# One layer of a hybrid decoder trunk: the q, k, sc_C and sc_x projections with stationary activations and blocks of quarters

## The chip, the core and the metric

One core of a Trainium2 chip runs the whole kernel in one launch. Its engines are TensorE (PE; the loading of its stationary operand has records of its own, PEld), VectorE (DVE), ScalarE (ACT), GpSimd (POOL) and SyncE (SP), which here only issues transfers. The metric is device time in microseconds (us), the median of three runs; lower is better.

## The reference

A batch of one, 256 tokens, 2048 channels, one layer, all in float32. What matters here:

```
h = rms_norm(x, norm_mix_g)                      # 256 x 2048
proj = h @ w_in                                  # 2048 x 14336
q, k, v, xr, gr, sc_b, sc_c, sc_x, g_pre = split(proj)   # 8 pieces of 1024, then 3 x 2048 gates
A = attention(q * 128**-0.5, k, v, rel_table)    # 8 heads of 128, causal, relative-position bias
B = rg_lru(conv4(xr)) * gelu(gr)                 # recurrence along the tokens
C = sc_b * conv3(sc_c * sc_x)                    # causal, per channel
m = sig(g_A) * (A @ w_attn_o) + sig(g_B) * (B @ w_lru_o) + sig(g_C) * (C @ w_sc_o)
x = x + m @ w_out
x = x + relu(rms_norm(x) @ w_up)**2 @ w_down     # 2048 -> 8192 -> 2048
return rms_norm(x) * final_g
```

## The kernel before

**Products in parts.** Each float32 number is split into a part `hi` in a shorter format (fp32r) and the rest `lo`; a product is hi·hi + hi·lo + lo·hi. The activations h are kept split (16 blocks `h0` to `h15` of 128 channels; the first 256 columns hi, the next 256 lo). Weights come from memory in tiles `raw` of 128x1024 (two blocks of 128 input channels by 512 output columns, 512 KB). One tile to be multiplied is called a job: `in_parts` writes hi by a copy on ACT and lo by a subtraction on DVE, both 128x1024, in a ring of WB = 5 buffers each. `ahead(n)` writes the program so that parts are made LOOK = 3 jobs ahead of the products.

**Two ways to multiply.** `group` (`ws`) keeps the weights stationary: for each 128x128 block of weights one matmul of 512 columns (hi against h in both parts) and one of 256 (lo against the hi part of h). A group is 512 output columns, 8 jobs; the result stands with channels on the partitions, its two parts are added (`total`: an ACT copy, a DVE addition, 256 columns each) and scaled by the norm's factor per token, `rsb`. `pair` (`as`) keeps the activations stationary and multiplies two groups at once: 12 matmuls of 512 columns per job, 16 jobs; the result stands with tokens on the partitions.

**Blocks of quarters.** In a pair, `nb` blocks of four jobs are multiplied by a scheme of seven products instead of eight (as Strassen's): `as_sequence` gives the order of the steps s1 to s7 and of the plain jobs n1, n2. Of such a block PE does seven half jobs (6 matmuls each) instead of four jobs (12 each); in return seven parts are made instead of four, and steps 2, 3, 4 and 6 first add two raw tiles on DVE (line 192). The stationary side of steps 2 to 5 needs sums of h, which `sums` makes on DVE and ACT (`h0c`, `h1c` and their parts). Steps 3 and 4 end in two more DVE operations (lines 309 and 310), and the final results of three of the four quarters need one more addition.

**Order of the work.** xr (two groups), q, k (two groups each, `ws`), v (a pair without quarters), sc_C, sc_x (`ws`), then for each branch its factor, the gates (`gt`, pairs with two blocks) and its output projection (`y`), then `wo`, and four times `up` and `dn`. Small work is written as generators put `beside` the products: `prepare` (tables for the bias: a matmul `pr`, its copy `rsbuf`, then through memory to POOL's tiles `rh` and `rl`, flipped by the matmuls `pf`), `recurrence`, `attention`, `h_sums`. `a_bit` runs one piece of the first generator in line, at most `pace` of them, and one entry of `after`, the rest of an evacuation (for xr: a multiplication by `rsb`, an ACT copy and three DVE multiply-adds for each of 8 pieces of the convolution). Only SP's order is the program's; that of the other engines is fixed when the program is built, by a scheduler. Each engine works off its own list in order.

Of the kernel before, what the change touches and what calls it, by code (L numbers as in the profile page):

```python
# [62 lines left out]
def trunk_kernel(ctx, tc, x8, xn, pv, rows, w_in, rel, onehot, w_a, lru_w, w_l, w_s, w_out, w_up, w_down, out2):  # L63
# [207 lines left out]
    def pair(name, w, g, plain, mix, evac, late=0):  # L271
# [41 lines left out]
        for n, s in enumerate(seq):  # L313
# [246 lines left out]
    pair("v", w_in, 4, lambda k, t: in_two(hl[k], t), None, evac)  # L560

    def attention():
        pt, pT = {}, {}
# [46 lines left out]
    hm = {}  # L610

    def h_sums():
        for b in range(NB_GATE):
            a = [block(f"ha{b}{i}") for i in range(2)]
            for i in range(4):
                h = hl[4 * b + i].bitcast(F32)
                dve.tensor_add(half(a, i), h[:, :S], h[:, S:])
            hm[b] = sums(f"h{b}", *a)
            yield

    beside(h_sums())
# [3 lines left out]
    sc = []
    for gidx in range(2):
        def evac(j, ps, gidx=gidx):
            g = 4 * gidx + j
            if g % 2 == 0:
                sc.append(block(f"sc{g}"))  # L630
            b = total(ps, f"sc{g}")
            dve.tensor_mul(half(sc, g), b, rsb)
        group(f"sc{gidx}", w_in, 12 + gidx, hl, evac)
    for gidx in range(2):
        def evac(j, ps, gidx=gidx):
            g = 4 * gidx + j
            b = total(ps, f"sx{g}")

            def rest():
                dve.tensor_mul(b, b, rsb)  # L640
                xp = u256(f"sp{g}", S + 2)
                dve.memset(xp[:, :2], 0.0)
                c = half(sc, g)
                dve.tensor_mul(xp[:, 2:], b, c)
# [289 lines left out]
```

## Time and profile before

| | |
|---|---|
| time, median of 3 runs (lowest, highest) | 1573.79 us (1573.08, 1576.48) |
| the profiled execution, its own time | 1573.67 us |
| its span, first to last instruction | 1571.9 us |
| PE busy | 1543.2 us (98%) |
| DVE busy | 1279.7 us (81%) |
| ACT busy | 878.5 us (56%) |
| mean granted TensorE clock | 0.997 |

The profiled execution's time is its span and 1.8 us around it, and 0.1 us below the median. PE's busy time holds the modelled ends of pipelined matmuls; how fast PE really goes is read from a run of matmuls without a gap.

### The profile page before, as it was taken

What the parts mean: (1) busy time and instruction counts of PE and PEld (TensorE: products, weight loads), DVE (VectorE), ACT (ScalarE), POOL (GpSimd) and SP (SyncE); (2) the same over time, 40 slices, a digit from 0 to 9 for tenths busy, and PEclk for the clock granted to TensorE, in tenths of its full rate; (3) what the DMA queues carried; (4) which work ended last, traced back from release to release, by engine and by line L of the source; (5) the groups of instructions that cost most, each with busy time, mean ns of one, the idle gap of its engine ahead of it and who ended that gap; (6) DMA issues with size and microseconds to landing.
All of it is one profiled execution on the core that took longest, in us unless ns stands there. A gap on an engine that the chain in (4) does not pass through costs nothing.

```text
span 1571.9 us, 20794 instructions
## 1 busy us (share of the span) xinstructions
PE 1543.2 (98%) x7684; PEld 1298.2 (83%) x7684; DVE 1279.7 (81%) x1649; ACT 878.5 (56%) x1172; POOL 57.2 (4%) x70
## 2 busy tenths in 40 slices
PE   8999999999999999999999999999999999999996
PEld 6888888878888888878788888888888888888885
DVE  6775566999769886989899778977799679976897
ACT  6555866565446454656557556545555446545554
POOL 1021200000000000200000000000000000000000
PEclk9999999999999999999999999999999999999998
DMA  9765555375755575473765654675467554666453
GB/s 360 254 196 170 162 189 160 121 271 160 245 182 175 188 268 183 135 268 128 262 202 187 214 189 139 208 254 188 134 214 252 187 185 171 195 236 209 145 183 112
DMA packets 87574, 309.77 MB, mean 197 GB/s; under 512 B 10269, under 2 KB 10533, under 8 KB 87472
## 3 DMA queue, kind: packets, MB, share of 16 engines
q1 hardware_dynamic: 83808, 298.67, 56.9%
q0 software_dynamic: 2656, 8.45, 1.9%
q8 instruction: 60, 0.98, 0.3%
q10 hardware_dynamic: 1008, 1.32, 0.2%
q14 instruction: 42, 0.34, 0.1%
HBM read 306.30 MB, written 2.11 MB: 196 GB/s over the span
## 4 chain that ended last, share of the span: by engine, by line
PE 84%; DVE 10%; issue 3%; DMA 1%; ACT 1%; POOL 0%; DVEq 0%; SPq 0%; POOLq 0%; ACTq 0%
PE dn L298 18%; PE up L251 15%; PE y L298 8%; PE up L252 8%; PE gt L298 8%; PE wo L298 5%; DVE lo L160 5%; PE qk L251 4%; PE v L298 3%; PE qk L252 2%; PE sc L251 2%; PE sx L251 2%; DVE raw L192 2%; PE xr L251 2%; PE sb L251 1%
## 5 line engine op out<-in xcount | busy, mean ns | idle before, releaser
L159 ACT ACTIVATE hi<-raw 128x1024 fp32r<-128x1024 f32 x648 | 667.4, 1056 | 554.1 <-DVE raw L192 115.5
L160 DVE TENSOR_TENSOR lo<-raw,hi 128x1024 fp32r<-128x1024 f32 x648 | 774.6, 1224 | 230.3 <-ACT hi L159 214.2
L251 PE MATMUL up<-h,hi 128*128 128x512 f32 x1024 | 360.5, 397 | 0.0
L252 PE MATMUL up<-h,lo 128*128 128x256 f32 x1024 | 287.5, 281 | 0.0
L251 PEld LDWEIGHTS up<-h,hi 128*128 128x128 f32 x1024 | 192.2, 188 | 46.4
L298 PE MATMUL dn<-hi,U 128*128 128x512 f32 x704 | 221.7, 389 | 0.4 <-ACT hi L159 0.4
L252 PEld LDWEIGHTS up<-h,lo 128*128 128x128 f32 x1024 | 193.5, 189 | 0.1
L298 PE MATMUL gt<-hi,h 128*128 128x512 f32 x528 | 167.9, 391 | 2.1 <-ACT hi L159 1.9
L298 PEld LDWEIGHTS dn<-hi,U 128*128 128x128 f32 x704 | 132.1, 188 | 28.6 <-ACT hi L159 0.8
L192 DVE TENSOR_TENSOR raw<-raw,raw 128x1024 f32<-128x1024 f32 x128 | 153.2, 1217 | 0.8
L298 PE MATMUL dn<-lo,U 128*128 128x512 f32 x352 | 137.2, 390 | 1.2 <-DVE lo L160 1.2
L298 PEld LDWEIGHTS gt<-hi,h 128*128 128x128 f32 x528 | 99.0, 188 | 23.9 <-ACT hi L159 2.9
L298 PE MATMUL gt<-lo,h 128*128 128x512 f32 x264 | 103.6, 392 | 3.0 <-DVE lo L160 3.0
L251 PE MATMUL qk<-h,hi 128*128 128x512 f32 x256 | 91.5, 401 | 0.0
L298 PEld LDWEIGHTS dn<-lo,U 128*128 128x128 f32 x352 | 66.1, 188 | 15.4 <-DVE lo L160 2.0
L252 PE MATMUL qk<-h,lo 128*128 128x256 f32 x256 | 71.7, 280 | 0.0
L298 PEld LDWEIGHTS gt<-lo,h 128*128 128x128 f32 x264 | 49.6, 188 | 16.0 <-DVE lo L160 5.6
L251 PEld LDWEIGHTS qk<-h,hi 128*128 128x128 f32 x256 | 48.1, 188 | 12.2 <-ACT hi L159 0.6
L251 PE MATMUL xr<-h,hi 128*128 128x512 f32 x128 | 45.3, 409 | 7.3 <-DVE h L379 6.7
L252 PEld LDWEIGHTS qk<-h,lo 128*128 128x128 f32 x256 | 48.3, 189 | 0.3
L251 PE MATMUL sc<-h,hi 128*128 128x512 f32 x128 | 46.6, 403 | 0.0
L251 PE MATMUL sx<-h,hi 128*128 128x512 f32 x128 | 45.9, 401 | 0.0
(899 smaller groups left out, 2315.9 us busy)
## 6 DMA issues: line engine op xcount, KB each, us to landing
raw<-in_w_in SPq DMA_DIRECT2D x222, 512.0 KB, 4.3
raw<-in_w_up SPq DMA_DIRECT2D x128, 512.0 KB, 4.3
raw<-in_w_down SPq DMA_DIRECT2D x128, 512.0 KB, 4.3
raw<-in_w_out SPq DMA_DIRECT2D x32, 512.0 KB, 4.5
raw<-in_w_a SPq DMA_DIRECT2D x16, 512.0 KB, 4.7
raw<-in_w_s SPq DMA_DIRECT2D x16, 512.0 KB, 5.3
raw<-in_w_l SPq DMA_DIRECT2D x16, 512.0 KB, 5.3
gb<-in_rows POOLq DMA_DIRECT2D x12, 256.0 KB, 4.6
```

Of the source, the lines that this page charges most:

```text
L159: act.activation(hi, raw, AF.Copy)
L160: dve.tensor_sub(lo, raw, hi.bitcast(F32))
L192: dve.tensor_add(t, t, add)
L251: pe.matmul(ps[j], hi[:, kk, cs], acts[k], start=(k == 0), stop=False)
L252: pe.matmul(ps[j][:, :S], lo[:, kk, cs], acts[k][:, :S], start=False, stop=(k == nk - 1))
L298: pe.matmul(ps[key], hl_[x], w2[y][:, kk], start=key not in begun, stop=end and i == 2, skip_group_check=True)
```

## The change

q, k, sc_C and sc_x go from `group` to `pair`, with 2, 1, 1 and 1 blocks of quarters; v gets one block. q and k come out with tokens on the partitions and are turned by `turned` (four 128x128 transposes on PE into one bank) and copied on ACT; the product of sc_C and sc_x is formed with tokens on the partitions and turned, too. The sums of h are formed beside the second half of xr's products, ahead of `prepare`, not beside sc_x's. In `as_sequence` step 7 stands behind step 4, with a plain job between steps 3 and 4; `dn` begins with its last plain jobs. There is one raw buffer less (8), six more blocks (49), and three small pools become one of 8.

```diff
-NBLK = 43
+NBLK = 49
-RAW = 9
+SMALL = 8
+RAW = 8
-NB_V, NB_Y = 0, 0
+NB_Q, NB_K, NB_V, NB_SC, NB_SX, NB_Y = 2, 1, 1, 1, 1, 0
...
+    units = list(range(2 * nb, nu))
+    if turn:
+        units = units[2:] + units[:2]
...
-    head = s[1] + n2[:a] + s[5] + s[2] + n2[a:-1] + s[3] + s[7] + s[4] + n2[-1:]
+    head = s[1] + n2[:a] + s[5] + s[2] + n2[a:-2] + s[3] + n2[-2:-1] + s[4] + s[7] + n2[-1:]
...
-    order = [("ws", w_in, g, 0, 8, 0) for g in (6, 7, 0, 1, 2, 3)]
-    order.append(("as", w_in, 4, 0, 8, NB_V))
-    for br, (w, gs) in enumerate(((w_a, (12, 13, 14, 15)), (w_s, (10, 11)), (w_l, (8, 9)))):
+    order = [("ws", w_in, g, 0, 8, 0) for g in (6, 7)]
+    order += [("as", w_in, g, 0, 8, nb) for g, nb in ((0, NB_Q), (2, NB_K), (4, NB_V), (12, NB_SC), (14, NB_SX))]
+    for br, (w, gs) in enumerate(((w_a, ()), (w_s, (10, 11)), (w_l, (8, 9)))):
...
+    def turned(name, o0, o1, j):
+        ps = small(name)
+        for q in range(2):
+            for th, src in ((0, o0), (1, o1)):
+                at = (2 * q + th) * P
+                pe.transpose(ps[:, at:at + P], src[:, (2 * j + q) * P:(2 * j + q + 1) * P], ident)
+        return ps
...
+    def h_sums():
+        for _ in range(4):
+            yield
+        for b in range(2):
...
+    beside(h_sums())
     A, B, C = [], [], []
     beside(prepare())
...
+        def evac(t, i, ps, other, op, which=which):
+            o = on[t, i] = block(f"qn{which}{t}{i}")
+            if other is not None:
+                dve.tensor_tensor(o, ps, other, op=op)
+                ps = o
+            act.activation(o, ps, AF.Copy, scale=rs1[:, S + t:S + t + 1] if which else rsq[:, t:t + 1])
...
+            def rest():
+                for j in range(2):
+                    n = 4 * which + 2 * i + j
+                    qk[n] = block(f"qk{n}")
+                    act.activation(qk[n], turned(f"pq{n}", o0, o, j), AF.Copy)
+            return rest
...
+        pair(f"qk{which}", w_in, 2 * which, lambda k, t: in_two(hl[k], t), hm, evac)
```

What moves on DVE at the beginning of q. The list of DVE before, from the fourth job of q on; `xc` is xr's convolution, `xp` its input:

```order
L498 SCALAR_TENSOR_TENSOR xc0_594<-xp0_591,pvt_77,xc0_594 128x256
L492 TENSOR_TENSOR xp1_659<-xr1b_374,rs1_166 128x256
L160 TENSOR_TENSOR lo19_673<-raw19_670,hi19_672 128x1024
L355 TENSOR_TENSOR xr6b_645<-xr1_2_402,xr6a_643 128x256
L498 SCALAR_TENSOR_TENSOR xc0_594<-xp1_659,pvt_77,xc0_594 128x256
L160 TENSOR_TENSOR lo20_679<-raw20_676,hi20_678 128x1024
```

And in the changed program, in the middle of q (jobs 25 to 30, steps 3 and 4; `raw21_01` and `raw22_01` are the raw tiles that step 4 adds to):

```order
L161 TENSOR_TENSOR lo25_808<-raw17_00_604,hi25_807 128x1024
L161 TENSOR_TENSOR lo26_820<-raw26_817,hi26_819 128x1024
L523 SCALAR_TENSOR_TENSOR xc4_776<-xp5_835,pvt_77,xc4_776 128x256
L193 TENSOR_TENSOR raw21_01_708<-raw21_01_708,raw19_11_673 128x1024
L523 SCALAR_TENSOR_TENSOR xc4_776<-xp5_835,pvt_77,xc4_776 128x256
L193 TENSOR_TENSOR raw22_01_729<-raw22_01_729,raw20_11_686 128x1024
L523 SCALAR_TENSOR_TENSOR xc4_776<-xp5_835,pvt_77,xc4_776 128x256
L161 TENSOR_TENSOR lo27_844<-raw21_01_708,hi27_843 128x1024
L161 TENSOR_TENSOR lo28_856<-raw22_01_729,hi28_855 128x1024
L310 TENSOR_TENSOR qk03_865<-qk0_10_847,qk0r1_698 128x512
```

The convolution, which stood among single subtractions, now stands among subtractions, additions of raw tiles and the ends of the steps.

The copy `rsbuf`, with which the tables for the bias begin, on DVE before (behind the eighth job of q):

```order
L160 TENSOR_TENSOR lo23_806<-raw23_803,hi23_805 128x1024
L498 SCALAR_TENSOR_TENSOR xc2_717<-xp3_766,pvt_77,xc2_717 128x256
L454 COPY rsbuf_775<-pr_773 8x384
L498 SCALAR_TENSOR_TENSOR xc2_717<-xp3_766,pvt_77,xc2_717 128x256
L160 TENSOR_TENSOR lo24_812<-raw24_809,hi24_811 128x1024
```

And in the changed program (behind step 6 of q, jobs 33 and 34; q's last job is 37):

```order
L193 TENSOR_TENSOR raw16_00_526<-raw16_00_526,raw29_10_876 128x1024
L193 TENSOR_TENSOR raw17_00_604<-raw17_00_604,raw30_10_894 128x1024
L574 TENSOR_TENSOR qn001_968<-qk0_01_715,qk03_865 128x512
L161 TENSOR_TENSOR lo33_942<-raw16_00_526,hi33_941 128x1024
L161 TENSOR_TENSOR lo34_953<-raw17_00_604,hi34_952 128x1024
L574 TENSOR_TENSOR qn011_971<-qk0_11_722,qk04_925 128x512
L464 COPY rsbuf_976<-pr_974 8x384
L161 TENSOR_TENSOR lo35_1007<-raw35_1004,hi35_1006 128x1024
```

It moved from the first half of q to its end, behind all of the convolution and all the additions.

DVE beside xr, before (the tenth and eleventh jobs; `sc8` are tiny operations of `prepare`):

```order
L355 TENSOR_TENSOR xr2b_386<-xr0_2_170,xr2a_384 128x256
L355 TENSOR_TENSOR xr3b_398<-xr0_3_171,xr3a_396 128x256
L442 TENSOR_SCALAR sc8_167<-sc8_167 128x8
L441 TENSOR_TENSOR sc8_167<-sc8_167 128x8
L442 TENSOR_SCALAR sc8_167<-sc8_167 128x8
L443 TENSOR_TENSOR sc8_167<-sc8_167 128x8
L160 TENSOR_TENSOR lo10_349<-raw10_346,hi10_348 128x1024
```

And in the changed program, at the same place:

```order
L365 TENSOR_TENSOR xr3b_381<-xr0_3_171,xr3a_379 128x256
L516 MEMSET xp0_579 128x3
L494 TENSOR_TENSOR ha00_437<-h0_98 128x256
L494 TENSOR_TENSOR ha00_437<-h1_105 128x256
L161 TENSOR_TENSOR lo10_332<-raw10_329,hi10_331 128x1024
L494 TENSOR_TENSOR ha01_438<-h2_115 128x256
L494 TENSOR_TENSOR ha01_438<-h3_121 128x256
L101 TENSOR_TENSOR h0c_443<-ha00_437 128x2x128
L99 TENSOR_TENSOR h0c_443<-ha00_437,ha01_438 128x2x128
L161 TENSOR_TENSOR lo11_393<-raw11_390,hi11_392 128x1024
```

The sums of h, 16 operations of 256 columns and two of 1024 in all, now stand between xr's ninth and last job.

## Rows read from the trace of the kernel before

**Rows 1.** The page, its first parts: span, busy time of the engines, and the granted clock in 40 slices of the span (tenths of full speed).

```profile
span 1571.9 us, 20794 instructions
PE 1543.2 (98%) x7684; PEld 1298.2 (83%) x7684; DVE 1279.7 (81%) x1649; ACT 878.5 (56%) x1172; POOL 57.2 (4%) x70
PEclk9999999999999999999999999999999999999998
```

**Rows 2.** Stretches of the span, in order: xr; q; k; v; sc_C; the first gates; sb; the fifth and the sixth pair of gates. Columns: stretch, its length, busy time (and count) of PE, PEld, DVE, ACT, POOL, granted clock, share of the DMA engines, GB/s.

```profile
0.00:55.70 55.70, 47.93 (x258) 40.67 (x259) 36.32 (x80) 37.66 (x68) 5.20 (x13) 1.00 0.95 351
55.70:104.60 48.90, 48.90 (x275) 41.69 (x274) 40.88 (x70) 25.89 (x38) 12.10 (x13) 1.00 0.64 201
104.60:153.50 48.90, 48.90 (x275) 42.67 (x274) 24.85 (x33) 23.75 (x37) 5.77 (x5) 1.00 0.56 176
153.50:198.90 45.40, 45.40 (x201) 37.57 (x201) 26.97 (x28) 35.66 (x51) 10.37 (x7) 1.00 0.54 170
198.90:253.20 54.30, 54.30 (x318) 46.96 (x316) 36.51 (x79) 34.41 (x71) 0.00 (x0) 1.00 0.53 169
303.20:346.60 43.40, 41.87 (x181) 33.38 (x180) 43.00 (x53) 27.29 (x32) 0.00 (x0) 1.00 0.57 188
431.00:476.30 45.30, 45.30 (x258) 39.24 (x257) 29.68 (x41) 19.51 (x27) 0.54 (x1) 1.00 0.55 174
647.00:694.30 47.30, 43.42 (x184) 33.69 (x183) 44.04 (x55) 29.27 (x43) 7.50 (x6) 1.00 0.58 193
715.80:761.90 46.10, 43.66 (x196) 34.94 (x195) 45.11 (x53) 30.02 (x35) 4.29 (x8) 1.00 0.60 211
```

**Rows 3.** The chain of work that ended last, in order of time: start, us, what (x how many). Of it: the matmul `pr`; the end of the first gates; two runs of products without a gap; eight transposes.

```profile
67.24 0.74 PE pr L452 x2
338.97 8.04 PE gt L298 x34
347.02 21.76 PE y L298 x96
368.78 40.80 PE gt L298 x180
869.72 0.87 PE px L784 x8
```

**Rows 4.** DVE in order of time, from 271 to 328 us, with rows left out: start, us, line, operation, operands, shape, x how many of them back to back.

```profile
271.08 1.42 DVE L617 TENSOR_TENSOR ha<-h 128x256 f32<-128x256 f32 x4
...
314.04 4.62 DVE L160 TENSOR_TENSOR lo<-raw,hi 128x1024 fp32r<-128x1024 f32 x4
318.58 3.49 DVE L192 TENSOR_TENSOR raw<-raw,raw 128x1024 f32<-128x1024 f32 x3
321.99 4.62 DVE L160 TENSOR_TENSOR lo<-raw,hi 128x1024 fp32r<-128x1024 f32 x4
326.53 0.68 DVE L309 TENSOR_TENSOR gt<-gt,gt00r 128x512 f32<-128x512 f32 x1
327.13 1.22 DVE L160 TENSOR_TENSOR lo<-raw,hi 128x1024 fp32r<-128x1024 f32 x1
```

**Rows 5.** DVE in order of time, 42 to 70 us, at the end of xr and in the first jobs of q, with rows left out; in brackets the idle time ahead of an operation and what ended it.

```profile
42.59 1.23 DVE L160 TENSOR_TENSOR lo<-raw,hi 128x1024 fp32r<-128x1024 f32 x1 [0.32 <-ACT hi L159]
...
44.86 1.23 DVE L160 TENSOR_TENSOR lo<-raw,hi 128x1024 fp32r<-128x1024 f32 x1 [0.77 <-ACT hi L159]
...
46.38 0.17 DVE L399 RECIPROCAL sc<-sc 128x2 f32<-128x2 f32 x1 [0.29 <-ACT sc L397]
...
47.33 1.23 DVE L160 TENSOR_TENSOR lo<-raw,hi 128x1024 fp32r<-128x1024 f32 x1 [0.20 <-ACT hi L159]
...
50.47 1.23 DVE L160 TENSOR_TENSOR lo<-raw,hi 128x1024 fp32r<-128x1024 f32 x1 [1.92 <-ACT hi L159]
...
53.09 0.42 DVE L492 TENSOR_TENSOR xp<-xr0b,rs 128x256 f32<-128x256 f32 x1 [1.40 <-ACT rs L409]
...
54.05 1.23 DVE L160 TENSOR_TENSOR lo<-raw,hi 128x1024 fp32r<-128x1024 f32 x1 [0.53 <-ACT hi L159]
...
69.09 0.54 DVE L454 COPY rsbuf<-pr 8x384 f32<-8x384 f32 x1
69.56 0.47 DVE L498 SCALAR_TENSOR_TENSOR xc<-xp,pvt,xc 128x256 f32<-128x256 f32 x1
69.95 1.20 DVE L160 TENSOR_TENSOR lo<-raw,hi 128x1024 fp32r<-128x1024 f32 x1
```

**Rows 6.** What PE waited for: engine, line and tile, the one waited for, us in all, times, longest.

```profile
PE gt L298 <- DVE lo L160: 4.1, 6, 1.1
PE gt L298 <- ACT hi L159: 2.6, 4, 1.0
PE gt L298 <- DVE gt L309: 0.9, 2, 0.7
PE wo L298 <- ACT MH L739: 0.3, 1, 0.3
```

**Rows 7.** POOL in order of time, from the write of the copy `rsbuf` to memory to the last table.

```profile
69.92 0.53 POOL L456 DMA_DIRECT2D rdram<-rsbuf  x1 [63.51 <-DVE rsbuf L454]
...
96.25 1.35 POOL L464 TENSOR_TENSOR rl<-rb,rh 128x512 fp32r<-128x512 f32 x1
```

**Rows 8.** The transposes `px` by tile: count, least/median/greatest duration in ns, first and last start.

```profile
L784 PE MATMUL px<-ident,xr x32: 270/272/273, 833.8 to 875.6; 128*128 128x128 f32 x32
```

More of the change, by code (lines that the diff above doesn't have):

```diff
@@ L335, in pair @@
             if n % 2:
-                a_bit()
+                a_bit(pace[0])
         if late:
@@ L473, in prepare @@
             yield
+    hm = {}
+    def h_sums():
+        for _ in range(4):
+            yield
+        for b in range(2):
+            a = [block(f"ha{b}{i}") for i in range(2)]
+            for i in range(4):
+                h = hl[4 * b + i].bitcast(F32)
+                dve.tensor_add(half(a, i), h[:, :S], h[:, S:])
+            hm[b] = sums(f"h{b}", *a)
+            yield
+    beside(h_sums())
     A, B, C = [], [], []
@@ L559, in evac @@
         vv[t, i] = o
-    pair("v", w_in, 4, lambda k, t: in_two(hl[k], t), None, evac)
+    pair("v", w_in, 4, lambda k, t: in_two(hl[k], t), hm, evac)
     def attention():
@@ L609, in trunk_kernel @@
     beside(attention())
[L610 to L621, printed above, removed]
-    pace[0] = 3
[L625 to L644, printed above, removed]
-                act.activation(c, xp[:, :S], AF.Copy, scale=col(C_SCW + g))
-                for m in range(1, 3):
-                    dve.scalar_tensor_tensor(c, xp[:, m:m + S], col(C_SCW + 8 * m + g), c, op0=OP.mult, op1=OP.add)
-            return rest
-        group(f"sx{gidx}", w_in, 14 + gidx, hl, evac)
+    pace[0] = 3
@@ new lines, in trunk_kernel, with evac, rest @@
+    sc, scn = [None] * 4, {}
+    def evac(t, i, ps, other, op):
+        o = scn[t, i] = block(f"scn{t}{i}")
+        if other is not None:
+            dve.tensor_tensor(o, ps, other, op=op)
+            ps = o
+        act.activation(o, ps, AF.Copy, scale=rs1[:, S + t:S + t + 1])
+    pair("sc", w_in, 12, lambda k, t: in_two(hl[k], t), hm, evac)
+    def evac(t, i, ps, other, op):
+        o = scn[t, i]
+        if other is not None:
+            x = block(f"sx{t}{i}")
+            dve.tensor_tensor(x, ps, other, op=op)
+            ps = x
+        dve.scalar_tensor_tensor(o, ps, rs1[:, S + t:S + t + 1], o, op0=OP.mult, op1=OP.mult)
+        if t == 0:
+            return
+        o0 = scn[0, i]
+        def rest():
+            for j in range(2):
+                n = 2 * i + j
+                px = turned(f"psx{n}", o0, o, j)
+                sc[n] = block(f"sc{n}")
+                for q in range(2):
+                    g = 2 * n + q
+                    xp = t256(f"sp{g}", S + 2)
+                    dve.memset(xp[:, :2], 0.0)
+                    act.activation(xp[:, 2:], px[:, q * S:(q + 1) * S], AF.Copy)
+                    c = half(sc, g)
+                    act.activation(c, xp[:, :S], AF.Copy, scale=col(C_SCW + g))
+                    for m in range(1, 3):
+                        dve.scalar_tensor_tensor(c, xp[:, m:m + S], col(C_SCW + 8 * m + g), c, op0=OP.mult, op1=OP.add)
+        return rest
@@ L650, in second_factor @@
+    pair("sx", w_in, 14, lambda k, t: in_two(hl[k], t), hm, evac)
     def second_factor():
```

35 lines of the change are left out of this document (16 added, 19 removed).

## Prediction

> **What bounds the kernel now.** I read the busy times first: PE 1543.2 of 1571.9 us, DVE 81%, ACT 56%, at the full clock almost everywhere [rows 1]. A kernel like this gets shorter only by less work on PE or by less idle time of PE, so the second view is the one by stretches [rows 2]: q, k, v, sc_C and sb have PE busy for their whole length. Idle time stands in xr (7.8 us) and in the pairs of gates: the first of them lasts from 303.2 to 347.02 [rows 2, 3], 43.8 us for products that take 40.80 without a gap in the second [rows 3], so 3.0 are lost; the fifth loses up to 6.5 (47.3) and the sixth 3.6 (46.1, less 40.8 and 16 transposes at 0.11). There DVE is busy 43.0 of 43.4, 44.0 of 47.3, 45.1 of 46.1: where a pair has two blocks of quarters and other work beside them, DVE is as long as PE. The waits say the same: PE waits for `lo`, which DVE makes, 4.1 us, and for `hi` 2.6 [rows 6]. In q DVE had 40.9 us of work in 48.9 [rows 2], and in k half of its time free. That contrast decides the case.
>
> **The change, part by part.**
>
> *PE, groups into pairs.* sb is two groups: 256 products in 45.3 us [rows 2]. A pair is 192 products; 96 without a gap took 21.76, 0.2267 each [rows 3], so 43.5. Four times 45.2 less 43.5 is 6.8 saved.
>
> *PE, six blocks of quarters.* A block saves one half job, 6 products, 1.36 us: 6 × 1.36 = 8.2 saved.
>
> *PE, turning.* 12 banks (four each for q, k and C) of four transposes: 48. Eight in a row took 0.87 [rows 3], 0.109 each: 5.2 added. PE's own sum is −6.8 − 8.2 + 5.2 = −9.8.
>
> *DVE in q.* Two blocks of quarters fall where xr's convolution still has to be worked off. I count DVE's list from the subtraction of q's first job (16) to the second subtraction of its last step 6 (job 34). Durations are distances between starts in rows of several: for 1024 columns (4.62 − 1.22)/3 = 1.13 [rows 4], for 512 327.13 − 326.53 = 0.60 [rows 4], for 256 (1.42 − 0.42)/3 = 0.335 [rows 4, 5], for a multiply-add 69.95 − 69.56 = 0.395 [rows 5].
>
> - 19 subtractions and 8 additions of raw tiles, 27 × 1.135: 30.6
> - 24 multiply-adds × 0.395: 9.5
> - 8 multiplications by `rsb` and 4 totals of 256, × 0.335: 4.0
> - 6 ends of steps of 512, × 0.60: 3.6
> - small ones: 0.5
>
> Together 48.2 us. PE, until it wants that last subtraction, has 5 plain jobs (12 × 0.2267 = 2.72) and 13 half jobs (1.36): 31.3, and `pr`, 0.74 at most [rows 3], of which I take 0.5: 31.8. What DVE has in hand decides the rest. Before, job 16's subtraction began at 47.33 [rows 5] and q's products at 55.70 [rows 2], 8.4 later. The sums of h now stand ahead of it: 16 × 0.335 + 2 × 1.135 = 7.6, against idle time of 0.32 + 0.77 + 0.29 + 0.20 = 1.6 [rows 5] there. So it begins at about 53.3, 2.4 ahead. PE's idle time in q: 48.2 − 2.4 − 31.8 = **14.0**. Bounds: 8.0 if the sums cost nothing of the lead (8.4 kept, by idle time further up or on ACT); 15 if DVE itself waits 1 us for raw tiles, of which there is a buffer less. I take 14.0, because DVE had nearly no idle time in the stretch of the same kind, 0.4 of 43.4 [rows 2]. It means that q, whose products need 41.5, ends near 111 and not at 97.
>
> Here a rule bears on the sum, and against the change. The row says that subtractions recorded as 1.22 start 1.13 apart [rows 4]. The Trainium skill, "VectorE: DVE Perf Modes", section "The DRAIN you can't avoid", says that the next operation does not start until the pipe of the one before is empty; the trace does not agree, by 0.09 us each. By the row DVE's list is 48.2; by the rule it would be some 6 longer (the fourth rival).
>
> *The first gates.* 3.0 lost before. Of the end of sx, 12 operations of 256 and 10 multiply-adds (4.0 + 4.0) stood between their subtractions; now it is 16 multiply-adds, 6.3, in one piece ahead of step 2. 1.7 less work on DVE, put close before the need: I take −1.0; bounds −3.0 (all of it) and +1.
>
> *Waits for turned results.* PE works in order, so a transpose whose input is not scaled yet holds the products behind it. Nearest row: `wo` for ACT's `MH`, 0.3 once [rows 6]. 12 banks: 0 to 3.6. In most cases several jobs lie between; I take +1.0.
>
> *At nothing.* The sums of h delay job 15 of xr, which PE wants only at the end of xr; the cover is the time from its subtraction (44.86 [rows 5]) to about 53, and without it each us counts fully. Step 7 behind step 4 leaves the number of DVE operations per block as it was. k, v, sc_C, sc_x get 2 more additions per step for one block each (8 × 1.135 + some ends, about 12 us), in stretches where DVE was busy 24.9 of 48.9, 27.0 of 45.4 and 36.5 of 54.3 [rows 2], and sx's convolution was there before.
>
> Sum: 1573.67 (the profiled execution) − 9.8 + 14.0 − 1.0 + 1.0 = **1577.9 us**, which is 4.1 above the median of the runs, 1573.79 (0.1 off the profiled one). 0.2%, 3.15 us, is about what a measurement of this kernel can tell from no change.
>
> **The rivals.**
>
> *The lead stays (q loses 8 or less).* For: ACT, not DVE, ended the idle times at the end of xr [rows 5], so the sums may fill time that my subtraction of 1.6 misses; and the convolution hangs on ACT too. Against: 7.6 us of work, however placed, in front of a list that is 16 longer than PE's. Time: 1577.9 − 6.0 = 1571.9.
>
> *Other side, the new order of the steps frees the gates.* Step 7 between step 4 and the next plain job gives DVE a half job more before the ends of steps 3 and 4 are wanted; if that is what the gates wait for, 3.0 + 6.5 + 3.6 = 13.1 us of idle time could go. For: PE waits for line 309's result [rows 6]. Against: 0.9 us only, and the second pair of gates with the old order lost nothing [rows 3]. It decides when more than 7.3 of the 13.1 go (1577.9 − 7.3 = 1570.6, faster by 0.2%); all of it gives 1565–1566.
>
> *The tables come late.* `rsbuf` was copied at 69.09 and POOL's last table was ready at 97.60, 28.5 later [rows 5, 7]. The copy now stands behind step 6's subtractions, at about 53.3 + 48.2 = 102, the last table at 130. PE wants the fourth in k about 23 us after k's start, 134 if q ends at 111: 4 us to spare. If q ends earlier without DVE's list being shorter up to the copy, or POOL is held by the recurrence, PE stands in k. Price 3 to 7: 1581–1585.
>
> *Operations that do not overlap.* If every DVE operation of q took its recorded length (1.23, 0.42, 0.47, 0.68 [rows 4, 5]), the list would grow by 27 × 0.095 + 12 × 0.085 + 24 × 0.075 + 6 × 0.08 = 5.9, which gives 1583.8; if transposes came singly, each at its 272 ns [rows 8], 48 × 0.163 = 7.8 more, 1585.7. Against both: the rows of several [rows 3, 4]. The first is what the Trainium skill's section above would make of q. Of the second the Trainium skill, "TensorE: Matmul & The Clock Gate", "Part 4: PE-mode transpose", gives about 275 ns for a transpose inside a kernel; the trace agrees for a single record, and not for eight in a row.
>
> **How the numbers follow.** Forecast (q starved by 11 to 15) 0.60, its own range 1573.5–1582 from the bounds of the small terms; the lead stays 0.15; the gates freed 0.10; late tables 0.11; no overlap 0.04. Range for 8 in 10: 1570–1584; it leaves out most of the freed gates and the ends of the last two. Faster by 0.2% (below 1570.6): 0.07 of the gates, 0.08 of the lead case together with small gains, 0.15. Slower (above 1576.9): 0.42 of the forecast (it stands 1.0 above the bound with ±4), 0.15 of tables and no overlap: 0.57. Within: 0.28.
>
> **What the profile of the changed kernel would show.** q about 55 us long with PE busy 42 and DVE without a gap; a wait of PE for `lo` (line 161) at `qk` of 10 us or more, first in step 2 of the second block; `rsbuf` copied at about 102 and no wait of PE at `pf`; runs of 192 − 6 nb products at 0.2267; four transposes in 0.44; the first gates 42 to 43 long. Wrong it is if q is under 50 us long, if PE waits in k for tables or turned results by more than 4 us, or if DVE in q has idle time while PE waits: then the wait is another's, ACT's or a transfer's.

## The result, and the profile after

The changed kernel takes 1594.27 us (median; 1593.61 to 1595.10), the kernel before 1573.43 beside it: a ratio of 1.0125, 95% interval 1.0112 to 1.0138. It is slower, as forecast, but by 20.8 us and not by 4: outside the range of 1570 to 1584.

The page, its first parts (answers to [rows 1]):

```profile
span 1591.9 us, 20372 instructions
PE 1549.9 (97%) x7440; PEld 1287.3 (81%) x7440; DVE 1327.6 (83%) x1659; ACT 896.5 (56%) x1188; POOL 56.6 (4%) x70
```

PE has 244 matmuls fewer than before and is recorded as busy for 6.7 us longer. Where the time goes, the stretches show (answers to [rows 2], same columns): xr; q; k; v; sc_C; sc_x; the first gates.

```profile
0.00:54.70 54.70, 47.47 (x258) 40.36 (x259) 41.15 (x92) 37.55 (x67) 5.21 (x13) 1.00 0.90 329
54.70:110.90 56.20, 48.07 (x187) 35.34 (x186) 56.05 (x85) 30.73 (x39) 1.27 (x2) 0.94 0.46 158
110.90:166.60 55.70, 51.86 (x224) 41.56 (x224) 35.90 (x32) 32.10 (x42) 18.23 (x15) 0.97 0.55 172
166.60:221.00 54.40, 51.15 (x225) 41.41 (x224) 35.86 (x35) 39.30 (x60) 11.18 (x8) 0.97 0.47 149
221.00:275.20 54.20, 53.18 (x255) 43.53 (x254) 49.45 (x91) 38.83 (x79) 1.14 (x2) 1.00 0.54 172
275.20:320.80 45.60, 45.60 (x211) 37.72 (x209) 36.39 (x49) 24.24 (x31) 1.08 (x2) 1.00 0.61 196
320.80:363.60 42.80, 42.53 (x192) 34.41 (x190) 42.31 (x53) 29.46 (x42) 0.00 (x0) 1.00 0.58 193
```

The table below gives the length of each stretch in the kernels that it takes to follow the argument, from the first product of one stage to the first of the next (us; e1 to e15 are the experiments below). Gates 1 to sb holds the first two pairs of gates and their output products, gr to wo the third branch; the last line goes from the first product of `dn` to its last. Left out are xr (1.1 shorter after than before), the second branch, the first `up` and the end, which hardly change. Where q and k are told apart, the border lies 18 products before the first turning transposes in k.

| | before | after | q plain | sums aside | spread | q, k groups | the best |
|---|---|---|---|---|---|---|---|
| run | | | e1 | e5 | e10 | e13 | e15 |
| q and k | 97.8 | 111.9 | 91.5 | 116.0 | 111.4 | 97.8 | 97.8 |
| v | 45.5 | 54.4 | 51.1 | 45.6 | 48.4 | 44.8 | 44.8 |
| sc_C | 54.1 | 54.2 | 58.2 | 56.7 | 60.1 | 61.8 | 54.9 |
| sc_x | 50.1 | 45.6 | 47.4 | 43.0 | 46.4 | 44.5 | 47.1 |
| gates 1 to sb | 127.9 | 127.1 | 127.4 | 128.0 | 127.3 | 128.7 | 127.1 |
| gr to wo | 181.9 | 183.0 | 182.9 | 182.2 | 182.9 | 183.5 | 181.5 |
| wo | 86.5 | 87.1 | 87.2 | 87.3 | 87.1 | 86.6 | 86.6 |
| first dn on | 600.3 | 602.1 | 602.1 | 602.1 | 602.1 | 600.3 | 600.3 |

So the 20 us are 7.3 in q (56.2 against 48.9), 6.8 in k, 8.9 in v, 1.1 in the third branch and 2.4 in wo and dn; sc_x and the first gates give 5 back and xr 1. In q DVE is busy 56.05 of 56.20 us: it is the bound there, as worked out. In k and v it is not (36 of 55): there something else is late.

What PE waited for (answers to [rows 6]; left out at the top are the wait at the kernel's start, 6.5 us here and 6.7 before, and 3.7 in the gates for `hi`, 2.6 before):

```profile
...
PE qk L299 <- DVE lo L161: 3.2, 3, 1.8
PE v L299 <- DVE lo L161: 3.0, 2, 2.6
PE qk L299 <- ACT hi L160: 2.8, 3, 1.3
PE pf L480 <- POOL rl L474: 2.3, 2, 1.9
PE gt L299 <- DVE lo L161: 1.7, 3, 1.2
PE pf L479 <- POOL rh L473: 1.6, 1, 1.6
...
PE pq L353 <- ACT qn L576: 1.2, 1, 1.2
```

The waits add up to less than the loss. PE in order of time in q, at step 2 of the two blocks, shows why:

```profile
63.90 0.50 PE L299 MATMUL qk<-hi,h0ch 128*128 128x512 f32 x1
66.17 0.50 PE L299 MATMUL qk<-lo,h0ch 128*128 128x512 f32 x1 [1.77 <-DVE lo L161]
...
68.89 0.79 PE L299 MATMUL qk<-lo,h1ch 128*128 128x512 f32 x1
69.48 0.63 PE L299 MATMUL qk<-hi,h1cl 128*128 128x512 f32 x1
```

From 63.90 to 66.17 is 2.27 us for one product of 0.23, so 2.04 were lost, of which 1.77 are called idle: the rest hides under the modelled end of the product before. And from 68.89 to 69.48 one product takes 0.59 instead of 0.23: the granted clock is 0.64 from 68 to 72, so for a part of this time it was at the lower of its two levels (1.2 and 2.4 GHz). Over q it is 0.94, over k and v 0.97 (the stretches above).

POOL from the copy's write to the last table (answers to [rows 7]):

```profile
101.97 0.53 POOL L466 DMA_DIRECT2D rdram<-rsbuf  x1 [95.55 <-DVE rsbuf L464]
...
114.10 2.13 POOL L474 TENSOR_TENSOR rl<-rb,rh 128x512 fp32r<-128x512 f32 x1
...
123.15 0.61 POOL L473 CAST rh<-rb 128x512 fp32r<-128x512 f32 x1 [6.22 <-DMA rb<-rdram]
123.85 2.18 POOL L474 TENSOR_TENSOR rl<-rb,rh 128x512 fp32r<-128x512 f32 x1
...
130.54 1.66 POOL L473 CAST rh<-rb 128x512 fp32r<-128x512 f32 x1 [3.83 <-ACT hi L160]
132.28 2.30 POOL L474 TENSOR_TENSOR rl<-rb,rh 128x512 fp32r<-128x512 f32 x1
...
139.49 1.29 POOL L474 TENSOR_TENSOR rl<-rb,rh 128x512 fp32r<-128x512 f32 x1
```

The copy came when the prediction said (102), but the chain from its write on took 38.8 us instead of 27.7, and the last table was ready at 140.8. Of the 11.1 us more, 3.7 are POOL's own operations (subtractions of 2.13 to 2.30 instead of 1.29, two casts of 1.7 instead of 0.6), and 7.4 are idle time of POOL, 22.7 instead of 15.2, mostly for transfers: `rb` landed 4.9 us after its issue (median; up to 6.8) instead of 3.6.

Last, v. ACT in order of time:

```profile
193.40 1.06 ACT L160 ACTIVATE hi<-raw 128x1024 fp32r<-128x1024 f32 x1 [0.30 <-PE v L299]
194.48 1.28 ACT L544 ACT_TABLE_LOAD   x1
195.78 0.91 ACT L544 ACTIVATE aa<-tt,sc 128x256 f32<-128x256 f32 x2
...
198.99 1.32 ACT L597 ACTIVATE vv<-vv,rs 128x512 f32<-128x512 f32 x2
...
202.62 0.90 ACT L545 ACTIVATE tt<-tt,sc 128x256 f32<-128x256 f32 x2
203.42 1.99 ACT L160 ACTIVATE hi<-raw 128x1024 fp32r<-128x1024 f32 x2
```

For 9 us ACT made no `hi`; all 16 exponentials and tangents of the recurrence and two scalings of v stood in one piece. Before, copies `hi` stood between them:

```profile
163.36 1.04 ACT L159 ACTIVATE hi<-raw 128x1024 fp32r<-128x1024 f32 x1
164.31 0.90 ACT L520 ACTIVATE tt<-tt,sc 128x256 f32<-128x256 f32 x2
...
165.91 1.04 ACT L159 ACTIVATE hi<-raw 128x1024 fp32r<-128x1024 f32 x1
```

In the changed kernel DVE was idle 6.3 us for want of `hi`, and then had everything at once:

```profile
204.49 2.36 DVE L161 TENSOR_TENSOR lo<-raw,hi 128x1024 fp32r<-128x1024 f32 x2 [6.32 <-ACT hi L160]
...
207.39 4.71 DVE L552 SCALAR_TENSOR_TENSOR tt<-aa,tt 128x512 f32<-128x512 f32 x4
```

PE stood 2.6 us, and the granted clock was 0.57 between 214 and 218.

### The profile page after: what moved, and what is told of

It is laid out like the page before. It is cut to its first block, busy times and chain, and to the rows that moved or that the text cites. A ratio compares the mean times of both kernels' runs of the same rounds, so it can differ in the third digit from the quotient of the medians.

```text
span 1591.9 us, 20372 instructions
## 1 busy us (share of the span) xinstructions
PE 1549.9 (97%) x7440; PEld 1287.3 (81%) x7440; DVE 1327.6 (83%) x1659; ACT 896.5 (56%) x1188; POOL 56.6 (4%) x70
## 4 chain that ended last, share of the span: by engine, by line
PE 81%; DVE 11%; ACT 3%; issue 3%; DMA 2%; POOL 1%; DVEq 0%; ACTq 0%; SPq 0%; POOLq 0%
PE dn L299 16%; PE up L252 15%; PE gt L299 12%; PE y L299 8%; PE up L253 8%; DVE lo L161 6%; PE wo L299 5%; PE sc L299 3%; PE qk L299 3%; PE sb L252 2%; PE gr L252 2%; DVE raw L193 2%; ACT hi L160 2%; PE v L299 2%; PE xr L252 1%
## 5 line engine op out<-in xcount | busy, mean ns | idle before, releaser
L160 ACT ACTIVATE hi<-raw 128x1024 fp32r<-128x1024 f32 x666 | 686.3, 1056 | 561.4 <-DVE raw L193 121.4
L161 DVE TENSOR_TENSOR lo<-raw,hi 128x1024 fp32r<-128x1024 f32 x666 | 797.4, 1225 | 228.5 <-ACT hi L160 227.1
L193 DVE TENSOR_TENSOR raw<-raw,raw 128x1024 f32<-128x1024 f32 x152 | 183.2, 1226 | 1.2
L299 PEld LDWEIGHTS gt<-hi,h 128*128 128x128 f32 x528 | 99.8, 190 | 24.3 <-ACT hi L160 3.8
L299 PE MATMUL qk<-hi,h 128*128 128x512 f32 x196 | 65.9, 408 | 1.6 <-ACT hi L160 1.6
L252 PE MATMUL xr<-h,hi 128*128 128x512 f32 x128 | 44.5, 406 | 6.8 <-DVE h L389 6.5
L299 PEld LDWEIGHTS qk<-hi,h 128*128 128x128 f32 x196 | 37.8, 194 | 10.4 <-ACT hi L160 2.5
L252 PE MATMUL sb<-h,hi 128*128 128x512 f32 x128 | 45.3, 399 | 0.0
L252 PE MATMUL gr<-h,hi 128*128 128x512 f32 x128 | 45.3, 399 | 0.0
L299 PE MATMUL qk<-lo,h 128*128 128x512 f32 x98 | 39.2, 400 | 0.7 <-DVE lo L161 0.7
L299 PE MATMUL y<-hi,B 128*128 128x512 f32 x128 | 39.7, 389 | 0.0
```

Of the source, the lines that this page charges most:

```text
L160: act.activation(hi, raw, AF.Copy)
L161: dve.tensor_sub(lo, raw, hi.bitcast(F32))
L193: dve.tensor_add(t, t, add)
L252: pe.matmul(ps[j], hi[:, kk, cs], acts[k], start=(k == 0), stop=False)
L299: pe.matmul(ps[key], hl_[x], w2[y][:, kk], start=key not in begun, stop=end and i == 2, skip_group_check=True)
```

## The experiments

**q's blocks.** First q without blocks (e1), and then all five pairs without (e2, a zero in each of the five places).

```diff
-NB_Q, NB_K, NB_V, NB_SC, NB_SX, NB_Y = 2, 1, 1, 1, 1, 0
+NB_Q, NB_K, NB_V, NB_SC, NB_SX, NB_Y = 0, 1, 1, 1, 1, 0
```

> The changed kernel (1594.3 us) with no block of quarters in q, the four other blocks and everything else kept. PE gets two half jobs more, 2.7 us. Theory A (DVE's overload in q is the root): q's idle time of 8.0 us, the lower clock behind it and with it the 15 us that q lasted over its products' time go, q lasts about 45 instead of 56.5; and since all later work is then less bunched, some of k's and v's loss goes too: 1571 to 1580. Rival B (the tables for the bias, and the recurrence in v, are late by their own place in the program): only q is mended, k still lasts 54 to 56 and v 53 to 55: 1582 to 1584.

1577.69 us, a ratio to before of 1.0021 (1.0012 to 1.0030): 16.6 less than the changed kernel. q and k of that run:

```profile
55.60:100.10 44.50, 44.50 (x197) 36.08 (x196) 38.83 (x65) 26.16 (x35) 0.00 (x0) 1.00 0.65 201
100.10:147.10 47.00, 47.00 (x214) 38.62 (x215) 32.54 (x31) 27.78 (x34) 12.92 (x14) 1.00 0.63 202
```

No idle time in either, the full clock in both: theory A for q and k. But in sc_C PE now waited 4.0 us for `lo`, once, so a part of what went came back later.

> The changed kernel with no block of quarters in q, k, v, sc_C and sc_x: the pairs, the transposes, the new order of steps in the later pairs and the early sums of h stay. PE gets 6 half jobs more than the changed kernel, 8.2 us. Theory A (the blocks' additional work on DVE starves PE): all of q to sx runs without idle time of PE beyond 2 us, and the time is the one of before less 6.8 for the pairs, plus 5.2 for the transposes, 1571 to 1574. Rival B (the recurrence and the tables bunch up because pairs drive the small work in another rhythm, half as many steps per job): k or v still show idle time and the lower clock, 1578 or more.

1583.80 us, 1.0065 (1.0049 to 1.0080). Theory A is wrong: without any block PE still waited 5.2 us for `lo` in sc_C, behind the recurrence. The four blocks in k to sc_x are worth 6.1 us (1583.8 − 1577.7), more than PE's 5.4 for them.

Then the same two blocks, but less beside them: the kernel leaves out three of the four taps of xr's convolution (e9).

```diff
-                for m in range(1, 4):
-                    dve.scalar_tensor_tensor(c, xp[:, m:m + S], col(C_LCW + 8 * m + g), c, op0=OP.mult, op1=OP.add)
```

> The changed kernel with the 24 multiply-adds of xr's convolution left out (of its four taps only the first, on ACT, is computed); all else, the two blocks in q too, is kept. It takes 24 x 0.395 = 9.5 us from DVE's list in q. Theory A (q's loss is DVE's list): q lasts 9 to 10 us less, 47 instead of 56.5, and loses 4 to 5 us, and the copy rsbuf comes 9 to 10 us earlier; whether k gains too depends on its start, which comes earlier by as much: 1583 to 1586 in all, with v's loss as before. Rival B (q waits for ACT or for raw tiles, of which there is one less): q lasts 53 us or more, 1591 or more.

1586.35 us, 1.0081 (1.0068 to 1.0095). Its q:

```profile
55.90:102.50 46.60, 43.95 (x187) 33.66 (x186) 46.51 (x61) 30.83 (x39) 1.26 (x2) 1.00 0.56 193
```

9.6 us less than 56.2, for 9.5 us (24 × 0.395) taken from DVE: q is as long as DVE's list. The copy `rsbuf` came 8.5 earlier, yet k was no shorter (57.6 against 55.7): PE reached it earlier too, and waited 4.8 us for the tables.

**The tables.** `pr`, `rsbuf` and POOL's chain beside xr, ahead of the sums of h, in a generator of their own (e4):

```diff
+    beside(tables())
     beside(h_sums())
```

> The changed kernel with the matmul pr, the copy rsbuf and POOL's chain for the bias tables issued beside xr, ahead of the sums of h; the flipping matmuls stay in k. In the changed kernel rsbuf was copied at 101.97 and the last table was ready 38.8 us later, and PE stood 3.9 us in k and ran some 6 us at a lower clock. Theory A (late tables are k's loss, q's is DVE's): k lasts about 49 instead of 55.4, q is as long as before this edit (56 to 57), in all 1587 to 1590. Rival B (k's loss follows from q's bunching of transfers and would come back as another wait): 1592 to 1595. If the copies on DVE beside xr cost q's lead, q gets longer by 1 to 2 us.

1596.52 us, 1.0141 (1.0127 to 1.0155): no gain, but the stretches tell it apart. q and k:

```profile
64.50:120.20 55.70, 46.93 (x184) 35.50 (x183) 55.29 (x83) 30.67 (x40) 0.00 (x0) 0.94 0.47 160
120.20:170.00 49.80, 49.60 (x225) 40.81 (x224) 34.47 (x32) 31.69 (x42) 3.70 (x4) 1.00 0.53 170
```

k takes 49.8 instead of 55.7 with its blocks and PE's and DVE's work as they were: late tables cost k 5.9 us. q is as it was. The gain went into xr, which lasted 9.8 us longer (58.0 against 48.2): PE waited 4.3 us there for `lo`. One piece of it is on record in the last section.

**The place in the queue.** The sums of h take six turns of the queue in which tables, recurrence and attention stand. Taken out of it (e5), and so with q plain (e6):

```diff
     def a_bit(n=1):
+        if early:
+            next(early[0], None)
...
-    beside(h_sums())
+    early.append(h_sums())
```

> The changed kernel with one edit: the sums of h are issued beside the same jobs of xr as before this edit, but in a queue of their own, so that they no longer take six turns from the queue in which the tables for the bias, the recurrence and the attention stand (a turn comes every second job, so these stood 12 jobs, some 30 us, later than in the kernel before). Theory A (this shift is what made k and v lose some 6 us each): the tables' copy comes back near 75 us, the recurrence falls in k and the first half of v, v's wait of 2.6 us and the lower clock behind it go, and q keeps its 14 us: 1581 to 1585. Rival B (the loss in k and v follows from the blocks in q, whatever the place of the tables): 1592 to 1596. A further wait is possible in q: the first flipping matmul stands 37 products behind pr, 8 us, and POOL needed 10 us for the first table.

1588.80 us, 1.0104 (1.0088 to 1.0120). q, k and v:

```profile
55.20:120.20 65.00, 52.60 (x197) 37.43 (x196) 61.84 (x86) 33.95 (x45) 14.90 (x13) 0.92 0.49 154
120.20:171.20 51.00, 50.86 (x231) 41.72 (x230) 29.74 (x30) 39.99 (x63) 7.66 (x8) 1.00 0.53 159
171.20:216.80 45.60, 44.51 (x203) 36.41 (x202) 43.96 (x45) 29.41 (x35) 6.86 (x4) 1.00 0.58 192
```

v is back at 45.6, so the shift did cost v its 8.8 us, and k is 4.7 shorter. But q is 8.8 longer: the flipping matmuls now stand in q and wait 4.8 us for POOL (3.1 and 1.7). The wait moved from k into q. v, sc_C and sc_x together take 145.3 us here and 154.2 in the changed kernel, so what v gained did not come back behind it.

> The sums of h in a queue of their own and no block of quarters in q. Theory A (two separate causes: DVE's overload in q, net of the two half jobs 12 us, and the shift of the queue, 12 us in k and v or, without q's blocks, 5 to 6 us in sc_C): against the 1577.7 of the kernel with q plain alone some 5 us less, 1571 to 1574. Rival B (the 4 us that PE waited in sc_C with q plain are the attention's and stay): 1576 to 1579.

1576.26 us, 1.0019 (1.0010 to 1.0028). Only 1.4 better than q plain alone, or 0.3 by the two ratios, so theory A's 5 us did not come: sc_C took 59.2 us, and PE waited 2.6 for the attention's `lgs`, made by DVE. Rival B.

Two more kernels with the sums aside have one block in q and the steps in their old order (e7), and in k two blocks as well (e8):

> The sums of h in a queue of their own, one block of quarters in q instead of two, and the order of the steps as in the kernel before (which alone cost 2.4 us there). DVE's list in q is then 19 operations of 1024, 21.6 us, 24 multiply-adds, 9.5, 12 of 256, 4.0, 3 of 512, 1.8: some 37 us against 40 of PE, so q should lose little. Theory A: 1.4 us less than with q plain for the block and 2.5 less for the order: 1566 to 1570, faster than the kernel before. Rival B (one block already starves PE in q, because additions and convolution come in one piece): q loses 4 to 6 us, 1571 to 1575.

> As the kernel with the sums aside, one block in q and the old order, and two blocks in k, where DVE has no convolution beside it. One half job less, 1.4 us, for DVE about 6 us more work in k. Theory A (DVE has room in k): 1 to 2 us less than with one block in k, 1565 to 1569. Rival B (the recurrence in k takes the room): 1 to 5 us more.

1589.17 us, 1.0101 (1.0084 to 1.0117), and 1586.54, 1.0083 (1.0068 to 1.0098). Neither theory: q and k took 110.3 and 108.6, of which 5.7 are waits of the flipping matmuls for POOL, which the list for DVE doesn't hold. These runs say nothing clean on one block in q.

**The lump in v.** The exponentials in four turns instead of two, in the changed kernel (e10):

```diff
-            if g % 4 == 3:
+            if g % 2 == 1:
                 yield
```

> The changed kernel with one edit: the recurrence's exponentials and tangents go in four turns of four instead of two turns of eight. In the changed kernel ACT worked off all sixteen and two scalings of v from 194.5 to 203.4 us without one copy hi, then DVE got its subtractions in one piece, and PE waited up to 2.6 us for lo and ran at the lower clock. In the kernel before, copies stood among them. Theory A (this lump is v's loss of some 6 us): v lasts 49 to 51 instead of 54.4, 1588 to 1591. Rival B (v's loss comes from DVE's share, the products with the recurrence's results, or from the start of the attention): v 53 or more, 1593 to 1595.

1596.37 us, 1.0144 (1.0129 to 1.0160). v and sc_C:

```profile
167.60:216.00 48.40, 48.17 (x220) 39.46 (x220) 30.88 (x31) 38.16 (x58) 6.40 (x6) 1.00 0.57 174
216.00:276.10 60.10, 55.19 (x254) 44.64 (x253) 53.85 (x90) 38.34 (x79) 5.94 (x5) 0.97 0.47 146
```

and, of what PE waited for, the longest but the one at the kernel's start, new here:

```profile
PE lg L609 <- DVE lgs L611: 4.3, 1, 4.3
```

v lost its 6.0 us, as theory A says, and sc_C took 5.9 more. The last operations of the recurrence on DVE stand in sc_C in both kernels (about 223 to 231). But the attention, two turns further back in the queue, began in sc_C, at 233.5, instead of in v, at 204.1, and its first `lgs` came on DVE at 239.7, behind the subtractions and additions of sc_C's block (DVE busy 53.85 of 60.1). So the lump explains 6.0 us of v, and spreading it gains nothing over the whole kernel.

**The order of the steps.** In the kernel before, the new order whole (e3), and of it only the turn of `dn`'s plain jobs, the last line (e11):

```diff
-    head = s[1] + n2[:a] + s[5] + s[2] + n2[a:-1] + s[3] + s[7] + s[4] + n2[-1:]
+    head = s[1] + n2[:a] + s[5] + s[2] + n2[a:-2] + s[3] + n2[-2:-1] + s[4] + s[7] + n2[-1:]
...
+        units = units[2:] + units[:2]
```

> The kernel before with one part of the change alone: the new order of steps (step 7 behind step 4, a plain job between steps 3 and 4, the output product of the MLP beginning with its last plain jobs). The changed kernel is 0.4 us longer in each of the four parts of the MLP's second product and 1.2 us in the pairs of gates behind gr than the kernel before. Theory A (the new order costs this): 1575 to 1577. Rival B (the order is neutral, and the raw buffer taken away or the small pool costs it): 1573 to 1574. Rival C (the order gains at the gates and the loss is another's): below 1572.

> The kernel before with only the second product of the MLP beginning with its last plain jobs; the steps in their old order. The new order as a whole cost 2.4 us there, 1.8 of them in the four parts of the MLP's second product. Theory A (the turned plain jobs alone cost it: a raw tile is fetched later for the blocks): 1575 to 1576. Rival B (step 7 behind step 4 costs it, since step 6 and the ends of steps 3 and 4 come closer together): 1573 to 1574.

1576.57 us, 1.0017 (1.0008 to 1.0025), and 1573.69, 0.9999 (0.9990 to 1.0008). So the steps' new order (step 7 behind step 4, a plain job between 3 and 4) costs 2.4 to 2.9 us over the whole kernel, 1.8 of it in `dn` (602.1 against 600.3), and the turn costs nothing. `dn`'s first pair is as long in both kernels (42.40, DVE busy 42.10 and 42.12); the loss comes behind it. The next 20 us after the change, and before:

```profile
1021.00:1041.00 20.00, 19.93 (x87) 15.83 (x86) 20.00 (x20) 11.57 (x13) 0.00 (x0) 1.00 0.43 131
1002.40:1022.40 20.00, 20.00 (x90) 16.57 (x89) 20.00 (x19) 12.58 (x13) 0.00 (x0) 1.00 0.43 135
```

DVE has no room in either, and PE begins three products fewer. Why the order does this, beyond DVE being full there, is not shown.

**What is left to gain.** All mends together, in the changed kernel: q plain, the sums aside, the recurrence in four turns, the steps in their old order (e12).

> All mends together: q as a pair without blocks, one block each in k, v, sc_C and sc_x, the sums of h in a queue of their own, the recurrence in four turns, the steps in the old order. Against the kernel with the sums aside and q plain (1576.3): 2.4 less for the order and 2 to 5 less for the waits of v and sc_C. Theory A: 1569 to 1572, faster than the kernel before by 0.1 to 0.3%. Rival B (the waits in sc_C are the attention's, whose DVE work stands beside a block of quarters, and stay): 1573 to 1575, no gain over the kernel before.

1575.72 us, 1.0007 (0.9998 to 1.0016): as fast as before, rival B; 2.0 us of wait for `lgs` stayed. Then q and k as groups again, with the sums of h aside, beside k, and the steps in their old order, so that only v, sc_C and sc_x are changed (e13 with a block in each of the three, e14 with one in sc_x alone):

> Only the part of the change behind k: q and k are groups as in the kernel before (so no turning of q and k, and no block beside xr's convolution), v, sc_C and sc_x are pairs with one block each, the sums of h stand in a queue of their own beside k, where DVE was busy half of the time; the steps in their old order. PE: two pairs for groups, 3 to 3.4 us less, 16 transposes, 1.8 more, three blocks, 4.1 less: 5.5 less. Theory A (the losses in v and sc_C of the changed kernel follow from the recurrence coming 12 jobs late and meeting the blocks of sc_C; here it stands where it stood before): v 44 to 45 and sc_C and sc_x together 99 to 100, 1568 to 1571, faster than the kernel before. Rival B (a block in v or sc_C cannot be fed beside recurrence and attention, wherever these stand): PE waits 3 to 6 us in v or sc_C, 1572 to 1576.

> As the kernel with q and k as groups, but with a block of quarters in sc_x alone, v and sc_C plain pairs: 2.7 us more for PE, some 11 us less for DVE in v and sc_C. Theory A (no loss in v and sc_C with the blocks either): 2 to 3 us slower than with the three blocks, 1571 to 1573. Rival B (the blocks in v and sc_C lose more than they save): as fast or faster than with the three, 1569 to 1573, with no wait of PE in v and sc_C.

1577.75 us, 1.0025 (1.0015 to 1.0035), and 1572.59, 0.9995 (0.9986 to 1.0004). sc_C with its block (e13):

```profile
198.10:259.90 61.80, 57.26 (x267) 46.34 (x266) 52.38 (x104) 42.00 (x87) 1.14 (x2) 0.97 0.47 145
```

its longest wait of PE:

```profile
PE pp L607 <- DVE lgs L597: 4.5, 1, 4.5
```

and sc_C without a block (e14):

```profile
199.20:252.20 53.00, 53.00 (x253) 43.38 (x251) 36.16 (x67) 33.94 (x67) 1.14 (x2) 1.00 0.51 163
```

sc_C is 8.8 us longer with its block, but a part of that is work moved: of the 88 matmuls recorded for the attention 80 stand in sc_C in e13 and 59 in e14, the others in sc_x. sc_C and sc_x together take 106.3 us in e13, 100.9 in e14 and 102.0 in e15 (below, also without it). So the block costs 4 to 5 us there instead of saving 1.4, even with the recurrence back in its old place; one in v saves 0.8 (44.8 against 45.6).

It is not the block alone. With the sums aside (e5) sc_C has the same block and all of the attention beside it, and PE has no idle time in it, 56.70 busy of 56.70 us; sc_C and sc_x together take 99.7. There the last operations of the recurrence on DVE ended at 209.1, before sc_C began at 216.8; in e13 they stand in its first part, at 203.7 to 210.7.

Last, blocks in v and sc_x alone, and a ninth raw buffer (e15; e16 has 43 blocks and ten small tiles):

```diff
-NBLK = 49
+NBLK = 47
...
-RAW = 8
+RAW = 9
```

> As the kernel with q and k as groups and a block in sc_x, with a block in v too (there it gained 0.8) and none in sc_C, and with nine raw buffers as before and 47 blocks. The stretch from gr to the output product was 1.2 to 2 us longer than in the kernel before in every kernel with eight raw buffers, in the old order of steps as well as in the new. Theory A (the raw buffer taken away costs that): 181.9 there again, 1569.5 to 1571, faster than the kernel before by 0.15 to 0.25%. Rival B (the one small pool costs it): 183 to 184 there, 1571.5 to 1572.5.

> The same with 43 blocks and ten small tiles in the one pool, as many as the three pools of the kernel before had. Theory A (raw buffers): as the kernel with eight small tiles, within 0.5 us. Rival B (the small pool): the stretch from gr to the output product back at 181.9 only here, 1569.5 to 1571. Fewer blocks can add a wait in v or sc_x: 1 to 3 us more.

1569.42 us, 0.9973 (0.9963 to 0.9983), and 1570.57, 0.9981 (0.9972 to 0.9990): both faster than the kernel before and the changed one. The third branch is back at 181.5 in both (183.7 in e14), so the raw buffer was what it lacked, not the small pool. v takes 44.8 in e15 and 45.9 in e16, so with 43 blocks its block of quarters gains nothing.

## Why the prediction was wrong

The sign and the place of the largest term were right, the size of the whole was not: 16 us are missing from the sum. The steps that failed are the price of the tables' chain and the terms put at nothing for the recurrence, the order of the steps and the raw buffer. Step by step:

- **PE's sum, −9.8.** About right where nothing waits. For the kernel with a block in v and sc_x the same prices give −3.4 for two pairs, −2.7 and +1.7, −4.4 in all; v to sb took 273.9 us against 277.6, 3.7 less. In the changed kernel itself sc_C and sc_x took 99.8 against 104.2, 4.4 less.
- **DVE in q, 14.0.** Right: 56.2 us against 42.2 for 180 products, `pr` and three transposes is 14.0, DVE was busy throughout, and taking 9.5 us from its list took 9.6 from q. The lower clock in q cost nothing extra, since DVE set the pace. The sign named for it was off: PE's recorded waits in q are 3.2 us for `lo` and 2.8 for `hi`, not 10 for `lo`, and begin in step 2 of the first block; the rest of the 14.0 stands in products that took longer. By the Trainium skill, "VectorE: DVE Perf Modes", "The DRAIN you can't avoid", as the prediction read it, DVE's list would have been some 6 longer; q shows no such time. The section itself adds that an operation that is not held starts earlier, which the prediction left out.
- **The first gates, −1.0.** 42.8 after 43.8, with 0.9 of turning transposes in it (8 × 0.109): −1.9.
- **Waits for turned results, +1.0.** Measured 1.2, once (`pq` for ACT's `qn`), in q.
- **The tables.** Here a step failed. They stood as a rival of 0.11, *instead of* the starved q, with 4 us to spare. They came on top of it. The copy came on time, at 101 to 102; the chain behind it was priced at 28.5 us, its duration in the kernel before, which would have ended at 130. It took 38.8 and ended at 140.8, 7 behind the 134 at which PE wants the fourth table; the sign "no wait of PE at `pf`" failed with 3.9. The larger part, 7.4 of the 11.1 us more, is transfers that landed later, the smaller one POOL's own operations beside DVE's (last section). Why the transfers took longer was not tried. A full DVE is not needed for a long chain: in e1 it took 35.1 us, with DVE busy 32.5 of 47.0 in k; there PE asked for the tables late enough and did not wait. Cost 5.9 (e4), within the 3 to 7 named for it.
- **"At nothing": the recurrence in v.** Not in the sum at all, and 6 to 9 us (e5, e10). That the sums of h, put ahead in the queue, move all that stands behind them by 12 jobs was seen for `rsbuf` alone. The prediction weighed how busy DVE was in v before (27 of 45) and not what would now stand there, and left out ACT, which made the gap.
- **"At nothing": step 7 behind step 4.** 2.4 us (e3). The number of operations was indeed the same; where they stand was not, in pairs in which DVE is busy 42.1 of 42.4 us. The prediction had this order only as a gain for the gates.
- **"At nothing": a raw buffer less.** 1.1 us in the third branch (183.0 against 181.9; 181.5 with nine again, e15).

The terms as measured, 1573.67 − 9.8 + 14.0 − 1.9 + 1.2 + 5.9 + 6.0 + 2.4 + 1.1 = 1592.6, stand 1.0 below the profiled 1593.61. That it closes so well is in part luck. With the 8.9 of e5 for the recurrence instead of the 6.0 of e10 it would be 1595.5, 1.9 above; the 1.2 lies inside q's 14.0 and counts twice; and xr, 1.1 shorter, is not in it. So it speaks for the list of terms, and not for the size of each.

What stays open: why exactly sc_C starves with a block in e13. The amount of DVE's work (52.4 of 61.8 us busy), the last operations of the recurrence in its first part, and the order in which the scheduler puts the attention's small operations were not tried apart. e5 speaks for the recurrence, but differs from e13 in q and k and in the order of the steps as well; and against it, in the changed kernel these operations stood in sc_C too (223.5 to 231.7), and PE waited only 1.0 there.

## What to carry to other kernels

An edit that puts work ahead in a shared queue moves everything behind it: list what stands there, and price each piece at its new place, on every engine that it uses. Rivals that can hold at the same time are to be added, not chosen between. A chain's duration holds for what stood beside it in its trace (here 27.7 us before and 38.8 after), so 4 us to spare behind such a chain is little. And where the saving is 1.4 us for six products, a place with room on the other engines is worth more than the number of blocks: the same scheme gains in v and sc_x (e15), loses in q, and in sc_C loses in one kernel (e13) and not in another (e5).

## What the runs showed of the hardware

POOL and DVE hold each other up. With the tables beside xr (e4), POOL's subtraction started just ahead of one on DVE:

```profile
38.76 1.28 POOL L453 TENSOR_TENSOR rl<-rb,rh 128x512 fp32r<-128x512 f32 x1
```

and DVE's of the same time, with the next of its kind:

```profile
38.81 2.31 DVE L161 TENSOR_TENSOR lo<-raw,hi 128x1024 fp32r<-128x1024 f32 x1
...
41.72 1.21 DVE L161 TENSOR_TENSOR lo<-raw,hi 128x1024 fp32r<-128x1024 f32 x1
```

DVE's took 2.31 instead of 1.21, longer by most of POOL's 1.28. The other way round, in the changed kernel, DVE's started just ahead of POOL's subtraction at 123.85:

```profile
123.66 1.23 DVE L161 TENSOR_TENSOR lo<-raw,hi 128x1024 fp32r<-128x1024 f32 x1 [1.09 <-ACT hi L160]
```

DVE's kept its length and POOL's took 2.18 instead of 1.29: 1.14 from the end of DVE's on. POOL's last one, at 139.49, with DVE idle until 140.60, took 1.29. One cast of the kernel with sums aside and q plain (e6) took 5.86 instead of 0.62:

```profile
95.43 5.86 POOL L475 CAST rh<-rb 128x512 fp32r<-128x512 f32 x1 [2.96 <-issue]
```

In that time DVE worked off five subtractions and additions of 1024 columns without a gap, the last of them until 100.8, each in its usual 1.21.

The Trainium skill, "SBUF — State Buffer", section "Who interferes with whom", says that a DVE instruction with two inputs in SBUF contends with a GpSimd instruction that reads SBUF, that the shared port pair is an exclusive lock, and that issue order decides who blocks. The rows with single operations agree: the one that started first kept its length. The cast of 5.86 was held up by a whole row of DVE's and not by one. In the prediction this would have made the chain of the tables longer, by some 3.7 us and not by all of the 11.1 measured.
